# Half-array matmuls emitted in pairs on different halves: SSD heads alternate by chunk, attention heads go two at a time

## The chip, the cores and the metric

The kernel runs on one core of one Trainium2 chip. The metric is device microseconds from start to end. PE is TensorE, a 128 x 128 array; DVE is VectorE, ACT is ScalarE, POOL is GpSimd. Before the change three runs took 4758.9, 4764.99 and 4768.86 us, so the median is 4764.99.

## What is computed

Two blocks of a transformer-like model on 512 tokens of 1024 features, in float32. The first block has chunk attention (8 heads of 64), an S5 state-space mixer, memory attention and an expert layer (PEER). The second block has two layers; each mixes an SSD (2 groups of 8 heads of 64), latent attention (MLA, 8 heads), a gated delta rule (GDN) and a feed-forward layer. The three parts that the change touches, cut:

```python
# chunk attention: 64 features a head, a relative bias, a mask by chunks
s = jnp.einsum('bnqhd,bnkhd->bhnqk', qc, kb) * (ATT_HEAD_DIM ** -0.5)
p = jax.nn.softmax(where(..., s + bias, NEG_INF), axis=-1)
o = jnp.einsum('bhnqk,bnkhd->bnqhd', p, vb)
...
# SSD, chunks of 128: within a chunk, and from the states before it; p = 64 features a head
y_diag = jnp.einsum('bcgls,bgecls,bcsgep->bclgep', CB, L, X)
y_off = jnp.einsum('bclgn,bcgepn,bgecl->bclgep', Cc, h_prev, jnp.exp(A_cum))
...
# MLA: 128 features of a head's own keys, 64 rotary ones shared by the heads
sc = (jnp.einsum('bqhd,bkhd->bhqk', qn, k_nope) + jnp.einsum('bqhr,bkr->bhqk', qp, k_pe))
pr = jax.nn.softmax(jnp.where(kpos[None, :] <= qpos[:, None], sc * scale, -jnp.inf), axis=-1)
o = jnp.einsum('bhqk,bkhd->bqhd', pr, v)
```

## The kernel before

Activations lie with features on partitions, as tiles of 128 x 512 tokens. Most of PE's work is products with weights ("gemm"): weights and activations are split into two float32r parts, and each chunk of 128 features takes three matmuls of 512 columns (L162 to L164). A weight tile's parts are made by ACT (L140) and DVE (L141).

The order of each engine's instructions is set by a scheduler from the program's order, by its own model of the times. Parts that shall overlap are written as generators, which are run in turn (`interleave`, `lockstep`). Buffers are handed out in program order: PSUM has 5 banks called `s`, 2 called `g` and 1 called `o`; `w2` is a ring of 8 tiles of 128 x 512 for intermediate values.

Three places use half of the array.

**SSD** (`Layer.ssd`). For each group, 4 pairs `k` of heads. A head's running decays are put on all partitions (`rows`, L1419, four passes in the trace); ACT makes four Relu (L1488) and two exp (L1489, L1491), DVE multiplies (L1490, L1492) into `e1` and `e2`; then seven matmuls for the four chunks (L1496 within a chunk, L1498 from the state before it), whose stationary operand has 64 columns and whose output is half of the pair's bank `py`: partitions 0 to 63 for head 0, 64 to 127 for head 1.

**Chunk attention** (`attention_head`). Two heads of a pair are interleaved. Scores (L701) contract 64 features, which lie on partitions 0 to 63 or 64 to 127; values (L706) write half of the pair's bank.

**MLA** (`Layer.mla`). A loop over 8 heads. Scores of a block of queries are a full matmul (L1574, 128 features) and one over the 64 rotary features (L1575) that lie on one or the other half of the partitions. Values (L1581) use the whole array.

Both attentions call `causal_probs`. It works on four blocks of 128 queries in the order 3, 0, 2, 1, with 512, 128, 384 and 256 keys; blocks 0 and 2 share a bank. It computes all scores, then DVE's reductions for the maximum (L274, L276), then ACT's exp (L281) and DVE's reciprocal and product (L282, L283), then PE's transposes (L249) and ACT's copies to the tile `pT` (L289).

Of the kernel before, what the change touches and what calls it, by code (L numbers as in the profile page):

```python
# [11 lines left out]
F32 = mybir.dt.float32  # L12
# [3 lines left out]
AF = mybir.ActivationFunctionType  # L16
# [4 lines left out]
NEG = -1e30  # L21
# [28 lines left out]
class Builder:  # L50
    """Pools, constants and the operations that the stages share.

    Activations lie with features on partitions: a tensor of 1024 features is
    eight tiles of [128, 512 tokens]."""

    def __init__(self, tc, d, ctx):
# [3 lines left out]
        # whether the split of weights goes before all other work  # L60
# [31 lines left out]
    def psg(self):  # L92
        """In turn one of three banks; of two where attention takes the third."""
# [9 lines left out]
    def consts(self):  # L103
# [8 lines left out]
        # tri[s, l] = 1 where s <= l  # L112
# [6 lines left out]
    def rsqrt(self, out, x, scale, eps):  # L119
        """out = (scale * x + eps) ** -0.5 by Newton's steps, for small tiles."""  # L120
# [35 lines left out]
    def mm3(self, ps, wH, wL, xs, start=True, stop=True):  # L156
        """ps (+)= w.T @ x over the chunks, each operand in two parts."""
# [8 lines left out]
    def gemm(self, ap, xs, n=T, ps=None):  # L166
        """ap: weights, or their parts where they have been loaded already."""
# [6 lines left out]
    def colsum(self, ps, acc, n=T):  # L174
        """ps[:, tb] = the sum over partitions of acc, tokens on partitions."""
# [4 lines left out]
    def rowbc(self, ps, col, n=T):  # L180
        """ps[p, t] = col[t % 128, t // 128] on every partition."""
# [17 lines left out]
    def rstd_rows(self, srcs, width, eps=EPS, n=T, w2=None, pss=None):  # L199
        """A PSUM tile with the tokens' reciprocal root mean squares on every partition."""  # L200
# [10 lines left out]
    def rstd_tile(self, srcs, width, eps=EPS, out=None):  # L211
        """The same on chip, until the next norm or in out."""
# [33 lines left out]
    def transpose4(self, ps, src, n=T):  # L246
        """ps[:, tb*128:...] = the transposes of src's blocks of 128 columns."""
# [5 lines left out]
    def causal_probs(self, score, mask, scale, pT):  # L253
# [4 lines left out]
        n = [(i + 1) * P for i in range(4)]  # L258

        def blocks(tile):  # L260
            # a block's columns in three tiles: the last, the first and third, the second
            a, b, c = tile(), tile(), tile()
            return [b[:, :P], c[:, :2 * P], b[:, P:], a]

        order = (3, 0, 2, 1)
        ps = blocks(self.pss)
        for i in order:
            score(ps[i], i)
# [1702 lines left out]
```

## Time and profile before

| | |
|---|---|
| median of three runs | 4764.99 us (4758.9 to 4768.86) |
| span of the profiled execution | 4766.1 us |
| mean granted TensorE clock, core 0 | 0.987 of full |
| PE busy | 4705.0 us, 99% of the span |
| DVE busy | 2838.4 us, 60% |
| ACT busy | 1907.6 us, 40% |

The page gives no time of the profiled execution apart from its span, which lies 1.1 us above the median of the runs. A busy PE is one that has a matmul in flight; it doesn't say how much of the array works. An fp32 matmul stands in the trace as two passes, so a count there is twice the program's; a float32r matmul is one. The time of a row includes the way through the array, so what one pass costs is read from start to start.

### The profile page before, as it was taken

The page shows a single profiled execution, that of the slowest core. Times are in us where ns is not written, and L with a number is a line of the kernel's source. Part 1 is how long each engine was busy: PE and PEld are TensorE (multiplying, and loading weights), DVE is VectorE, ACT ScalarE, POOL GpSimd, SP SyncE. Part 2 cuts the span into 40 slices and gives each one's busy share as a digit, 9 for nine tenths or more (in the row PEclk, how much of TensorE's full clock was granted, in tenths as well). Part 3 has the DMA queues.
Part 4 walks back from the last instruction along what each step waited for, and adds up shares of the span by engine and source line. Part 5 has one row for each costly group of instructions (what it writes and reads, how often), then busy time and mean ns, then how long its engine had stood idle before and what let it go on. Part 6 is the DMA issues. An engine that isn't in the chain of part 4 may idle for free.

```text
span 4766.1 us, 59356 instructions
## 1 busy us (share of the span) xinstructions
PE 4705.0 (99%) x22296; PEld 3754.0 (79%) x22296; DVE 2838.4 (60%) x5744; ACT 1907.6 (40%) x3653; POOL 29.1 (1%) x59
## 2 busy tenths in 40 slices
PE   8999999999999999999999999999999999999998
PEld 6777788888888888887787678888877876888887
DVE  8655799665545555557776545544477764555434
ACT  3343348863222222323553433333345534333322
POOL 0000000000000000000000000000000000000000
PEclk9789999999999999999999999999999999999999
DMA  4222235564434443442254145423323531554332
GB/s 131 66 84 83 80 118 186 190 210 150 138 119 139 143 129 126 145 138 74 85 178 137 45 154 175 146 93 96 104 81 127 174 103 52 176 167 133 93 95 82
DMA packets 306048, 589.28 MB, mean 124 GB/s; under 512 B 60192, under 2 KB 147552, under 8 KB 303584
## 3 DMA queue, kind: packets, MB, share of 16 engines
q1 hardware_dynamic: 304480, 582.88, 37.7%
q0 software_dynamic: 1280, 2.59, 0.3%
q8 instruction: 176, 2.88, 0.2%
q14 instruction: 112, 0.92, 0.1%
HBM read 480.29 MB, written 105.09 MB: 123 GB/s over the span
## 4 chain that ended last, share of the span: by engine, by line
PE 91%; DVE 6%; DMA 1%; issue 1%; ACT 0%; SPq 0%; DVEq 0%; ACTq 0%
PE g L162 14%; PE g L163 14%; PE g L164 14%; PE o L163 6%; PE o L164 6%; PE o L162 6%; PE s L1170 5%; PE s L1171 5%; PE s L1169 5%; PE s L1116 3%; PE s L249 1%; DVE wL L141 1%; PE s L1575 1%; PE s L1574 1%; PE s L183 1%
## 5 line engine op out<-in xcount | busy, mean ns | idle before, releaser
L140 ACT ACTIVATE wH<-wr 128x1024 fp32r<-128x1024 f32 (+2 forms) x599 | 603.3, 1007 | 1305.3 <-PE g L163 794.9
L141 DVE TENSOR_TENSOR wL<-wr,wH 128x1024 fp32r<-128x1024 f32 (+2 forms) x599 | 692.2, 1156 | 444.4 <-ACT wH L140 428.6
L162 PE MATMUL g<-xH,wH 128*128 128x512 f32 (+1 forms) x2328 | 923.4, 397 | 16.7 <-ACT wH L140 13.7
L164 PE MATMUL g<-xH,wL 128*128 128x512 f32 (+1 forms) x2328 | 919.9, 395 | 6.6 <-DVE wL L141 6.5
L163 PE MATMUL g<-xL,wH 128*128 128x512 f32 (+1 forms) x2328 | 922.2, 396 | 0.0
L162 PEld LDWEIGHTS g<-xH,wH 128*128 128x128 f32 x2328 | 444.7, 191 | 118.9 <-ACT wH L140 14.0
L164 PEld LDWEIGHTS g<-xH,wL 128*128 128x128 f32 x2328 | 444.4, 191 | 106.8 <-DVE wL L141 10.9
L163 PEld LDWEIGHTS g<-xL,wH 128*128 128x128 f32 x2328 | 444.7, 191 | 95.3 <-issue 3.7
L164 PE MATMUL o<-xH,wL 128*128 128x512 f32 x1032 | 411.2, 398 | 1.5 <-DVE wL L141 1.5
L163 PE MATMUL o<-xL,wH 128*128 128x512 f32 x1032 | 412.4, 400 | 0.0
L162 PE MATMUL o<-xH,wH 128*128 128x512 f32 x1032 | 411.2, 398 | 0.0
L1170 PE MATMUL s<-WL,VH 128*128 128x512 f32 x1024 | 399.7, 391 | 1.3 <-DVE WL L141 1.3
L1169 PE MATMUL s<-WH,VH 128*128 128x512 f32 x1024 | 398.2, 391 | 0.0
L1171 PE MATMUL s<-WH,VL 128*128 128x512 f32 x1024 | 397.7, 390 | 0.0
L140 ACT ACTIVATE VH<-vr 128x1024 fp32r<-128x1024 f32 x128 | 132.3, 1056 | 542.9 <-PE s L1170 391.4
L1172 DVE TENSOR_TENSOR h<-h,s 128x512 f32<-128x512 f32 x256 | 174.1, 685 | 271.6 <-PE s L1171 271.5
L164 PE MATMUL g<-yH,wL 128*128 128x512 f32 x632 | 251.0, 397 | 2.3 <-DVE wL L141 2.3
L163 PE MATMUL g<-yL,wH 128*128 128x512 f32 x632 | 251.1, 397 | 0.7 <-DVE yL L230 0.7
L162 PE MATMUL g<-yH,wH 128*128 128x512 f32 x632 | 250.5, 397 | 0.0
L141 DVE TENSOR_TENSOR VL<-vr,VH 128x1024 fp32r<-128x1024 f32 x128 | 154.1, 1224 | 141.4 <-ACT VH L140 141.3
L164 PEld LDWEIGHTS o<-xH,wL 128*128 128x128 f32 x1032 | 194.6, 189 | 45.2 <-DVE wL L141 2.4
L162 PEld LDWEIGHTS o<-xH,wH 128*128 128x128 f32 x1032 | 194.5, 188 | 44.5 <-issue 2.2
(629 smaller groups left out, 7243.3 us busy)
## 6 DMA issues: line engine op xcount, KB each, us to landing
wr<-in_w_in SPq DMA_DIRECT2D x166, 512.0 KB, 3.6
wr<-in_pu SPq DMA_DIRECT2D x128, 512.0 KB, 4.2
vr<-in_pv SPq DMA_DIRECT2D x128, 512.0 KB, 3.7
gd<-G SPq DMA_DIRECT2D x16, 2048.0 KB, 6.5
gt<-gd SPq DMA_DIRECT2D x64, 512.0 KB, 5.3
wr<-in_w_o SPq DMA_DIRECT2D x64, 512.0 KB, 3.6
wr<-in_w_up SPq DMA_DIRECT2D x64, 512.0 KB, 3.5
wr<-in_w_dn SPq DMA_DIRECT2D x64, 512.0 KB, 3.5
```

Of the source, the lines that this page charges most:

```text
L140: nc.scalar.activation(H, src, AF.Copy)
L141: nc.vector.tensor_tensor(L, src, f32(H), op=OP.subtract)
L162: nc.tensor.matmul(ps, wH[:, k], xH, start=s, stop=False)
L163: nc.tensor.matmul(ps, wH[:, k], xL, start=False, stop=False)
L164: nc.tensor.matmul(ps, wL[:, k], xH, start=False, stop=e)
L183: self.nc.tensor.matmul(ps[:, tb * P:(tb + 1) * P], col[:, tb:tb + 1].to_broadcast([P, P]), self.ident, start=True, stop=True)
L249: self.nc.tensor.transpose(ps[:, tb * P:(tb + 1) * P], src[:, tb * P:(tb + 1) * P], self.ident)
L1116: nc.tensor.matmul(ps[:, j * P:(j + 1) * P], o2[:, k], og[:, j], start=True, stop=True)
L1169: nc.tensor.matmul(ps, VH[:, n], WH, start=k == 0, stop=False)
L1170: nc.tensor.matmul(ps, VH[:, n], WL, start=False, stop=False)
L1171: nc.tensor.matmul(ps, VL[:, n], WH, start=False, stop=k == 3)
L1172: nc.vector.tensor_tensor(h[n], h[n], ps, op=OP.add)
```

## The change

The SSD first prepares both heads of a pair, then goes through the chunks, and for each chunk and each of the two products issues head 0 and head 1 one after the other (L1523 for both). `causal_probs` takes two heads. For each block it issues the scores of both heads and right behind them, in the program, DVE's reductions of both; since blocks 0 and 2 share a bank, block 2's scores follow the reductions of block 0 there. The exp and the normalisation work in place, in the tiles that the reductions wrote. `attention_head` becomes `attention_pair`: scores on both row halves (L719), values on both column halves in turn (L727). The MLA takes its heads two at a time: full-array scores of both (L1604), then the rotary ones of both on the two row halves (L1608), values L1615. `qn`, `kn`, `vt` get 3 buffers in place of 2, the tiles `pT` 2 in place of 3. Comments are removed too, so line numbers shift; L274, L276, L281, L282, L283 and L289 become L282, L284, L292, L293, L294 and L300.

```diff
     def causal_probs(self, score, masks, scale, pTs):
-        ps = blocks(self.pss)
-        for i in order:
-            score(ps[i], i)
-        yield
...
-        s = blocks(self.w2)
+        ps, s, pt = blocks(self.pss), blocks(self.w2), blocks(self.pss)
+        mx, nmx, sm, ri = ([self.small([P, 4]) for _ in R2] for _ in range(4))
         for i in order:
             c = slice(i, i + 1)
-            nc.vector.tensor_tensor_reduce(out=s[i], in0=ps[i], in1=mask[:, T - n[i]:], scale=1.0,
...
+            score([ps(h, i) for h in R2], i)
+            for h in R2:
+                nc.vector.tensor_tensor_reduce(out=s(h, i), in0=ps(h, i), in1=masks[h][:, T - n[i]:], scale=1.0,
+                                               scalar=-3e38, op0=OP.add, op1=OP.max, accum_out=mx[h][:, c])
+                nc.vector.tensor_scalar(nmx[h][:, c], mx[h][:, c], -scale, None, op0=OP.mult)
+            if i == 0:
+                yield
+        yield
+        for h in R2:
+            for i in order:
+                c = slice(i, i + 1)
+                p = s(h, i)
+                nc.scalar.activation(p, p, AF.Exp, bias=nmx[h][:, c], scale=scale, accum_out=sm[h][:, c])
...
+            yield
+        for h in R2:
+            for i in order:
+                self.transpose4(pt(h, i), s(h, i), n[i])
...
 def attention_pair(B, qT, kT, vt, j, out, pool):
...
+    for k in range(4):
+        for h in R2:
+            lo = 64 * h
+            n = 64 * (2 * j + h)
+            nc.tensor.matmul(out[lo:lo + 64, k * P:], vt[:, k, n:n + 64], pTs[h][k], start=k == 0, stop=k == 3)
...
     def ssd(self, xs, xr, rs, decays, px, pool):
...
-                    for c in range(4):
-                        sl = slice(c * P, (c + 1) * P)
-                        o = py[64 * e:64 * e + 64, sl]
-                        nc.tensor.matmul(o, xd[:, c, 64 * hd:64 * hd + 64], e1[:, sl], start=True, stop=c == 0)
-                        if c:
-                            nc.tensor.matmul(o, st[c - 1][:, 64 * hd:64 * hd + 64], e2[:, sl],
-                                             start=False, stop=True)
+                    e1s.append(e1)
+                    e2s.append(e2)
+
+                for c in range(4):
+                    sl = slice(c * P, (c + 1) * P)
+                    for lhs, rhs, first in ((xd[:, c], e1s, True), (st[c - 1] if c else None, e2s, False)):
+                        for e in range(2):
+                            if lhs is not None:
+                                hd = 2 * k + e
+                                nc.tensor.matmul(py[64 * e:64 * e + 64, sl], lhs[:, 64 * hd:64 * hd + 64],
+                                                 rhs[e][:, sl], start=first, stop=c == 0 or not first)
...
     def mla(self, xs, gates, pool):
...
+            def score(pss, i):
+                sl, n = slice(i * P, (i + 1) * P), (i + 1) * P
+                for h in R2:
+                    nc.tensor.matmul(pss[h], qn[h][:, sl], kn[h][:, :n], start=True, stop=False)
+
+                for h in R2:
+                    lo = 64 * h
+                    nc.tensor.matmul(pss[h], qpe[lo:lo + 64, sl], kpe[lo:lo + 64, :n], start=False, stop=True)
```

How PE's order moves is shown at three places; a row gives line, operation, out<-in, and the shape of the output (partitions x columns), with what it waits for in brackets where it waits.

PE before, in the MLA's first layer: the scores of the first head (banks `s`; `kn` and `qn` are its keys and queries, `kpe` and `qpe` the rotary ones).

```order
L1574 MATMUL s_22120<-kn_22062,qn_22061 128x512 [waits PE_49]
L1575 MATMUL s_22120<-kpe_22013,qpe_22029 128x512
L1574 MATMUL s_22121<-kn_22062,qn_22061 128x128 [waits PE_49]
L1575 MATMUL s_22121<-kpe_22013,qpe_22029 128x128
L1574 MATMUL s_22121<-kn_22062,qn_22061 128x384
L1575 MATMUL s_22121<-kpe_22013,qpe_22029 128x384
L1574 MATMUL s_22122<-kn_22062,qn_22061 128x256
L1575 MATMUL s_22122<-kpe_22013,qpe_22029 128x256
```

PE after, at the same place: the first pair of heads, up to the third block of queries.

```order
L1604 MATMUL s_22164<-kn_22039,qn_22038 128x512 [waits PE_49]
L1604 MATMUL s_22165<-kn_22097,qn_22096 128x512
L1608 MATMUL s_22164<-kpe_21990,qpe_22006 128x512
L1608 MATMUL s_22165<-kpe_21990,qpe_22006 128x512
L1604 MATMUL s_22176<-kn_22039,qn_22038 128x128
L1604 MATMUL s_22177<-kn_22097,qn_22096 128x128 [waits PE_49]
L1608 MATMUL s_22176<-kpe_21990,qpe_22006 128x128
L1608 MATMUL s_22177<-kpe_21990,qpe_22006 128x128
L1604 MATMUL s_22196<-kn_22039,qn_22038 128x256 [waits DVE_49]
L1604 MATMUL s_22176<-kn_22039,qn_22038 128x384 [waits DVE_49]
L1604 MATMUL s_22177<-kn_22097,qn_22096 128x384 [waits DVE_49]
L1608 MATMUL s_22176<-kpe_21990,qpe_22006 128x384
```

Each block has its two full matmuls first and then its two rotary ones; the third block (384 columns) writes the banks of the second, `s_22176` and `s_22177`, and waits for DVE.

PE before, behind those scores: gemm rows for the next head's products (`g_22201`, `g_22221`) and the transposes (L249) of the normalised probabilities.

```order
L164 MATMUL g_22201<-cqH_21819,wL_22198 128x512
L162 MATMUL g_22201<-cqH_21825,wH_22197 128x512
L163 MATMUL g_22201<-cqL_21826,wH_22197 128x512
L249 MATMUL s_22161<-ident_65,w_4763_22146 128x128 [waits DVE_49]
L249 MATMUL s_22161<-ident_65,w_4763_22146 128x128 x3
L249 MATMUL s_22162<-ident_65,w_4764_22147 128x128 [waits DVE_49,PE_49]
L164 MATMUL g_22201<-cqH_21825,wL_22198 128x512
L162 MATMUL g_22221<-ckvH_21935,wH_22217 128x512
L163 MATMUL g_22221<-ckvL_21936,wH_22217 128x512
L164 MATMUL g_22221<-ckvH_21935,wL_22218 128x512
L249 MATMUL s_22163<-ident_65,w_4765_22148 128x128 [waits DVE_49]
L249 MATMUL s_22162<-ident_65,w_4764_22147 128x128 [waits Activation_49]
```

PE after, behind the last scores of the pair: the transposes of head 0's blocks 3 and 0 (`s_22232`, `s_22241`), gemm rows, and the transposes of its block 1 (`s_22250`) and of head 1 (`s_22255`).

```order
L249 MATMUL s_22232<-ident_65,w_4758_22170 128x128 [waits DVE_49]
L249 MATMUL s_22232<-ident_65,w_4758_22170 128x128 x3
L249 MATMUL s_22241<-ident_65,w_4762_22182 128x128 [waits DVE_49]
L164 MATMUL g_22303<-cqH_21789,wL_22300 128x512
L162 MATMUL g_22303<-cqH_21795,wH_22299 128x512
L163 MATMUL g_22303<-cqL_21796,wH_22299 128x512
L164 MATMUL g_22303<-cqH_21795,wL_22300 128x512
L162 MATMUL g_22303<-cqH_21801,wH_22299 128x512
L163 MATMUL g_22303<-cqL_21802,wH_22299 128x512
L164 MATMUL g_22303<-cqH_21801,wL_22300 128x512
L249 MATMUL s_22250<-ident_65,w_4766_22202 128x128 [waits DVE_49]
L249 MATMUL s_22250<-ident_65,w_4766_22202 128x128
```

Seven gemm rows stand ahead of the first transposes before, and none after; after, seven stand between the first head's block 0 and its block 1. Behind the pair's values come 48 gemm rows.

PE before, in the SSD: the end of one head and the gemm rows behind it.

```order
L1496 MATMUL s_18882<-w_4084_18906,xd_18697 64x128
L1498 MATMUL s_18882<-w_4085_18907,st_18746 64x128
L1496 MATMUL s_18882<-w_4084_18906,xd_18697 64x128
L1498 MATMUL s_18882<-w_4085_18907,st_18753 64x128
L164 MATMUL g_19402<-xH_18306,wL_19399 128x512
L162 MATMUL g_19402<-xH_18312,wH_19398 128x512
L163 MATMUL g_19402<-xL_18313,wH_19398 128x512
L164 MATMUL g_19402<-xH_18312,wL_19399 128x512
L162 MATMUL g_19402<-xH_18318,wH_19398 128x512
L163 MATMUL g_19402<-xL_18319,wH_19398 128x512
```

PE after: the third pair of a group. The first row of head 0 stands ahead of the `rows` (L1440) of the next pair, and the others alternate between head 0 (`w_4050`, `w_4051`) and head 1 (`w_4053`, `w_4054`).

```order
L1523 MATMUL s_18816<-w_4050_18820,xd_18673 64x128 [waits DVE_49]
L1440 MATMUL s_18859<-cumTH_18580,eye_14191 128x512 [waits PE_49]
L1440 MATMUL s_18859<-cumTL_18581,eye_14191 128x512
L1440 MATMUL s_18872<-cumTH_18580,eye_14191 128x512 [waits PE_49,Activation_49]
L1440 MATMUL s_18872<-cumTL_18581,eye_14191 128x512
L164 MATMUL g_19027<-xH_18294,wL_19024 128x512
L1523 MATMUL s_18816<-w_4053_18833,xd_18673 64x128 [waits DVE_49]
L1523 MATMUL s_18816<-w_4050_18820,xd_18673 64x128
L1523 MATMUL s_18816<-w_4053_18833,xd_18673 64x128 [waits Activation_49]
L1523 MATMUL s_18816<-w_4051_18821,st_18716 64x128
L1523 MATMUL s_18816<-w_4054_18834,st_18716 64x128
L1523 MATMUL s_18816<-w_4050_18820,xd_18673 64x128
```

The two heads' rows stand next to each other now, and few gemm rows are left between pairs. On PE as a whole the number of instructions of each line stays as it is.

## Rows read from the trace of the kernel before

**Rows 1.** The page, part 1: busy us, share of the span, instructions.

```profile
PE 4705.0 (99%) x22296; PEld 3754.0 (79%) x22296; DVE 2838.4 (60%) x5744; ACT 1907.6 (40%) x3653; POOL 29.1 (1%) x59
```

**Rows 2.** The page, part 4: the chain that ended last, by engine.

```profile
PE 91%; DVE 6%; DMA 1%; issue 1%; ACT 0%; SPq 0%; DVEq 0%; ACTq 0%
```

**Rows 3.** Windows: length, then PE, PEld, DVE, ACT, POOL busy, granted clock, DMA.

```profile
2270.00:2290.00 20.00, 20.00 (x109) 15.36 (x108) 13.38 (x21) 12.23 (x30) 0.00 (x0) 1.00 0.15 44
2660.00:2700.00 40.00, 40.00 (x166) 25.41 (x165) 20.44 (x72) 19.94 (x67) 0.00 (x0) 1.00 0.11 34
60.00:360.00 300.00, 289.74 (x1542) 218.01 (x1543) 190.40 (x654) 116.51 (x276) 21.50 (x40) 0.85 0.28 81
2240.00:2800.00 560.00, 555.89 (x2603) 419.84 (x2602) 375.17 (x759) 261.35 (x586) 1.26 (x1) 1.00 0.36 115
```

**Rows 4.** Timeline of PE, MLA values: start, us to the last end, line, shapes, count.

```profile
2651.96 2.32 PE L1581 MATMUL s<-pT,vt 128*128 128x512 f32 x8
2654.04 0.48 PE L164 MATMUL o<-ckvH,wL 128*128 128x512 f32 x1
```

**Rows 5.** Timeline of PE, one head of the SSD.

```profile
2267.97 0.65 PE L1496 MATMUL s<-w,xd 128*64 128x128 f32 x4
2268.46 0.38 PE L1498 MATMUL s<-w,st 128*64 128x128 f32 x2
2268.68 0.38 PE L1496 MATMUL s<-w,xd 128*64 128x128 f32 x2
...
2269.65 0.49 PE L1419 MATMUL s<-cumTH,eye 24*128 24x512 f32 x1
...
2270.76 0.50 PE L163 MATMUL g<-xL,wH 128*128 128x512 f32 x1
```

**Rows 6.** Timeline of PE, S5's alternating column halves and the matmul behind them.

```profile
106.92 1.15 PE L623 MATMUL s<-U,inj 128*64 128x64 f32 x32
108.00 0.50 PE L162 MATMUL g<-xH,wH 128*128 128x512 f32 x1
```

**Rows 7.** Timeline of PE, GDN's matmuls of 64 columns and the one behind.

```profile
2815.87 0.68 PE L1751 MATMUL s<-tt,a 64*64 64x64 f32 x8
2816.47 0.50 PE L164 MATMUL o<-xH,wL 128*128 128x512 f32 x1
```

**Rows 8.** Timeline of PE, S5's matmuls on the two row halves.

```profile
124.42 0.32 PE L651 MATMUL s<-x,car 64*128 64x64 f32 x1
124.44 0.32 PE L652 MATMUL s<-x,cai 64*128 64x64 f32 x1
```

**Rows 9.** Timeline of PE, one MLA head's scores, first rows, and the matmul behind.

```profile
2641.16 1.02 PE L1574 MATMUL s<-kn,qn 128*128 128x512 f32 x2
2642.11 1.12 PE L1575 MATMUL s<-kpe,qpe 64*128 64x512 f32 x2
...
2646.94 0.50 PE L163 MATMUL g<-cqL,wH 128*128 128x512 f32 x1
```

**Rows 10.** Timeline of DVE and ACT for the same head.

```profile
2643.28 0.69 DVE L274 CUSTOM_DVE_ANT_0 w<-s,cmask 128x512 f32<-128x512 f32 x1 [1.22 <-PE s L1575]
...
2644.01 0.15 DVE L276 TENSOR_SCALAR sm<-sm 128x1 f32<-128x1 f32 x1
2644.20 0.72 ACT L281 ACTIVATE w<-w,sm 128x512 f32<-128x512 f32 x1 [3.59 <-DVE sm L276]
...
2645.79 0.29 DVE L274 CUSTOM_DVE_ANT_0 w<-s,cmask 128x128 f32<-128x128 f32 x1 [1.62 <-PE s L1575]
...
2649.30 0.94 ACT L289 COPY pT<-s 128x128 f32<-128x128 f32 x5 [0.52 <-PE s L249]
```

**Rows 11.** Timeline of ACT in the SSD.

```profile
2270.41 1.14 ACT L1488 ACTIVATE w<-s,cum 128x128 f32<-128x128 f32 x4 [2.44 <-PE s L1419]
...
2272.31 1.17 ACT L1488 ACTIVATE w<-s,cum 128x128 f32<-128x128 f32 x4
2273.38 1.06 ACT L140 ACTIVATE wH<-wr 128x1024 fp32r<-128x1024 f32 x1
```

More of the change, by code (lines that the diff above doesn't have):

```diff
@@ L250, in transpose4, with causal_probs, at @@
                                      self.ident)
-    def causal_probs(self, score, mask, scale, pT):
+    def causal_probs(self, score, masks, scale, pTs):
         nc = self.nc
         n = [(i + 1) * P for i in range(4)]
+        order = (3, 0, 2, 1)
+        R2 = range(2)
         def blocks(tile):
-            a, b, c = tile(), tile(), tile()
-            return [b[:, :P], c[:, :2 * P], b[:, P:], a]
-        order = (3, 0, 2, 1)
-        ps = blocks(self.pss)
-        for i in order:
-            score(ps[i], i)
-        yield
-        mx, nmx, sm, ri = (self.small([P, 4]) for _ in range(4))
-        s = blocks(self.w2)
+            made = [{} for _ in R2]
+            def at(h, i):
+                t = {3: 0, 0: 1, 2: 1, 1: 2}[i]
+                if t not in made[h]:
+                    made[h][t] = tile()
+                x = made[h][t]
+                return {3: x, 0: x[:, :P], 2: x[:, P:], 1: x[:, :2 * P]}[i]
+            return at
+        ps, s, pt = blocks(self.pss), blocks(self.w2), blocks(self.pss)
+        mx, nmx, sm, ri = ([self.small([P, 4]) for _ in R2] for _ in range(4))
@@ L293, in prob_tiles @@
+    def prob_tiles(self, pool, bufs):
         t = self.t([P, 10 * P], F32, "pT", bufs, pool)
@@ L810, in heads @@
                 ps = B.t([P, T], F32, "o", 1, B.pp)
-                yield from interleave([attention_head(B, *pairs[j], vt, 2 * j + k, ps, pool) for k in range(2)], 2)
+                yield from attention_pair(B, *pairs[j], vt, j, ps, pool)
                 att.append(B.t([P, T], F32, "qk", 8, pool))
@@ new lines, in mla, with score @@
+        R2 = range(2)
+        for j in range(4):
+            qpe = t([P, T], "qpe", 2)
+            self.rope(qpe, B.gemm(B.d["w_uq2"][self.l, 8 + j], cq))
+            qn, kn, vt = [], [], []
+            for h in (2 * j, 2 * j + 1):
+                qn.append(t([P, T], "qn", 3))
+                kn.append(t([P, T], "kn", 3))
+                nc.scalar.copy(qn[-1], B.gemm(B.d["w_uq2"][self.l, h], cq))
+                nc.scalar.copy(kn[-1], B.gemm(B.d["w_ukv2"][self.l, h], ckv))
+                f = B.w2()
+                nc.scalar.copy(f, B.gemm(B.d["w_ukv2"][self.l, 8 + h], ckv))
+                ps = B.pss()
+                B.transpose4(ps, f)
+                vt.append(t([P, T], "vt", 3))
+                v.tensor_copy(vt[-1], ps)
+            pTs = [B.prob_tiles(pool, 2) for _ in R2]
+            def score(pss, i):
+                sl, n = slice(i * P, (i + 1) * P), (i + 1) * P
+                for h in R2:
+                    nc.tensor.matmul(pss[h], qn[h][:, sl], kn[h][:, :n], start=True, stop=False)
+                for h in R2:
+                    lo = 64 * h
+                    nc.tensor.matmul(pss[h], qpe[lo:lo + 64, sl], kpe[lo:lo + 64, :n], start=False, stop=True)
+            for _ in B.causal_probs(score, [S.cmask] * 2, scale, pTs):
+                pass
+            for h in R2:
+                ps = B.pss()
+                for k in range(4):
+                    nc.tensor.matmul(ps[:, k * P:], vt[h][:, k * P:(k + 1) * P], pTs[h][k],
+                                     start=k == 0, stop=k == 3)
+                H, L = B.hl("y")
+                B.split(ps, H, L)
+                out.append((H, L))
```

81 lines of the change are left out of this document (23 added, 58 removed).

## The prediction

> **What bounds the kernel now.** I read the page's busy shares first. TensorE (PE) is busy for 99% of the span, VectorE (DVE) 60%, ScalarE (ACT) 40% [rows 1], and the chain that ended last is 91% PE [rows 2]. So nearly everything PE gives up comes off the end, as long as it finds other work ready. Next I looked at the stages that are changed. In 20 us of the SSD, DVE works 13.4 and ACT 12.2; in 40 us of the latent attention (MLA), 20.4 and 19.9; PE is never idle there, and the clock is at its full level, 2.4 GHz, over the long stretches that hold both stages [rows 3]. DVE and ACT have room on average, but not much if their work is bunched. Only the stage of chunk attention and S5 (60 to 360 us) has a mean clock of 0.85.
>
> The span is 4766.1 us, the runs' median 4765.0; I subtract from 4765. Their spread is 10 us, about 0.2%: less than 9.5 us can't be told from no change.
>
> **What a half-array matmul costs now.** An fp32 matmul is two passes in the trace. In the MLA, four full-array `L1581` (512, 384, 256 and 128 columns, 8 passes) take 2651.96 to 2654.04: 2.08 us [rows 4]. One head's SSD matmuls step by 0.22 us for two passes of 128 columns on half the array [rows 5], which is also what two passes of 128 columns cost on the whole array by the first figure (2.08 x 2/20). Half an array is no faster; the other half idles.
>
> **Do two halves work at once?** The trace has a case: `L623` of S5 alternates the column halves, 32 passes of 64 columns. The next matmul starts 1.08 us after its start [rows 6], 34 ns for each pass, with the change of tile shape in it. Eight passes of 64 columns of `L1751` that don't alternate take 0.60 us, about 0.05 each after 0.2 for the change [rows 7]. So alternating passes go about two by two. For row halves: an `L651` and an `L652` on different halves and banks start 0.02 us apart [rows 8], though each runs for longer than that.
> The Trainium skill, "TensorE: Matmul & The Clock Gate", section "Part 3: Packing small matmuls", says that a weight load overlaps with running matmuls only where the row group differs; column halves share their rows. By that rule the SSD and `L706` would gain nothing, 26.6 us of the sum below. The 34 ns of `L623` speak against it, and the sum goes by the row. It remains a rival.
>
> **What a change of tile shape costs.** One MLA head's scores go from 2641.16 to 2646.94, 5.78 us, over eight instruction pairs that alternate whole array (`L1574`) and row half (`L1575`) [rows 9]. Their columns are those of two `L1581` groups, 4.16 us. The other 1.62 us are eight changes: 0.20 each.
>
> **The change, part by part.**
> SSD: 2 layers x 16 heads, 14 passes each [rows 5], 28 for a pair of heads; x 0.11 = 3.08 us. In the new order the first row of one head stands apart in 14 of 16 pairs; it costs its 0.22, and then the other half's seven rows bound the rest, 1.54: 1.76 in all, 1.32 less. 14 x 1.32 + 2 x 1.54 = **21.6 us**.
> MLA rope scores (`L1575`, now `L1608`): 16 heads x 2.08 = 33.3, all adjacent in pairs in the new order: half, **16.6**.
> Chunk attention scores (`L701`, now `L719`): 8 heads x 2.08 = 16.6 at full clock, adjacent too: **8.3**. Values (`L706`, now `L727`): the first row (512 columns, 0.83 us) of one head stands apart in every pair, so a pair of heads takes 0.83 + 2.08 in place of 4.16, 1.25 less, x 4 = **5.0**. Both run in the stretch with a clock of 0.85; their passes cost more there, up to 2 us together. I take the lower figure, since the clock may change as well.
> Changes of shape: counted down the two orders, 495 before and 415 after. 61 of the 80 are those between whole array and row halves (107 each way, now 76 and 77), nearly all in the MLA: 8 a pair of heads for 16. 61 x 0.20 = 12.2. The others lie at column halves: a head of the SSD leaves 0.14 us over its 14 passes when the rows of the next one start (2267.97 to 2269.65), so 19 x 0.15 = 2.9. Together **15.1**.
> Gross: 21.6 + 16.6 + 8.3 + 5.0 + 15.1 = 66.6 us.
>
> **New waits, MLA.** The third score (384 columns) now goes into the bank of the second, after DVE has reduced it. By the durations of before [rows 10]: the 512-column reduction and the small operation that ends at 2644.16 are 0.88 us together, the 128-column reduction 0.3. DVE does the 512 ones of both heads before the 128 ones, so the bank comes free some 2.1 us after the first scores end; PE has left by then the change, the 128-column scores (0.9 with their changes) and one 256-column `L1604` (0.42), 1.5 in all. Wait: 0.6.
> Then the transposes. Before, 7 gemm rows and more stand between scores and transposes and a single head's softmax follows. Now both heads' softmax must run at once, on ACT the exp of eight blocks (0.72 for 512 columns), on DVE eight reductions and eight normalisations behind one another. PE has two transposes' worth and 7 gemm rows (1.6 us) before it needs the last block of the first head. Following the queues of DVE and ACT with those durations, that block is ready 0.55 to 1.2 us after PE gets there; I take 0.9. The value products wait for ACT's copies out of PSUM (0.19 each), by up to 0.4; I take 0.3. Together 1.8 us for a pair of heads, x 8 = **14.4**. Behind PE's wait stand the next gemms, whose results are not needed for some 10 us (48 gemm rows follow a pair's values), so nothing else becomes late. Bounds: 0, if DVE and ACT run ahead, and double.
>
> **New waits, SSD.** A head costs ACT about 1.9 us (four Relu, two exp; from one `L1488` to the next, 2270.41 to 2272.31) [rows 11]. Before, 11 gemm rows stood between heads; now 0 to 5 stand between pairs, so the pairs of a group follow one another at ACT's pace. PE's own work for a pair is 2 x 1.11 (`L1419`, 2269.65 to 2270.76) + 1.76 + 0.3, and a gemm row or so, 4.5 to 5 us; ACT's 3.8, with a weight cast (1.06) up to 4.9. They are close, and what shows is the latency at the first and the last pair: about 1 us at each, 2 a group, 4 groups, **8 us**. Bounds: 0 and 16.
>
> **Sum:** 66.6 - 14.4 - 8 = 44 us; 4765 - 44 = **4721 us**.
>
> **Rivals.**
> A. The waits stay hidden: DVE and ACT run ahead of what I follow, and PE waits 0 to 8 us in all. For it: both work 50 to 70% of the time in these stages [rows 3]. Against it: the scores, the softmax that they need and the transposes stand next to each other in the new order, with 7 gemm rows to cover it. About 4699 us.
> B. Column halves run one after the other, for the rule above: 26.6 us are lost, and SSD's waits shrink by some 4: 4744.
> C. The softmax of two heads is a longer chain than I follow, for every hand-over between DVE and ACT adds to it, and a pair waits twice as long, 14 us more in all; so does the SSD, 8 more: 4743.
> D. Slower: in the MLA PE falls to the lower level of its clock, 1.2 GHz. Place: the stretch from 2639 to 2775 and its twin in the second layer, 136 us each, where PE would have new pauses and fewer rows busy. What speaks for it: between 60 and 360 us the clock is 0.85 in the mean, in a stage where gemms mix with short and half-array matmuls [rows 3]. Against it: both stretches ran at 1.00, with a pause at every change of shape. At half clock a stretch costs its own length more; from about 45 us of it in all the change loses. With half of both stretches, 136 us, 4857; with a quarter, 4789.
> E. The halves never run together, row halves neither: only the 15.1 us of changes against 22 of waits, 4772.
>
> **How the numbers follow.** Forecast (4709 to 4732) 0.50; A 0.20; B and C together 0.19; E 0.05; D 0.04; the last 0.02 is for a better clock in the first stage (by the mean of 0.85 some 90 of the 300 us ran at the lower level; a third of them at full clock would save 15). The range 4692 to 4750 reaches to A and past B and C, and leaves out D, E and the ends. Faster by over 0.2% in the forecast, A, nearly all of B and C: 0.88; within 0.2%: most of E and the tail of C, 0.07; slower: D and part of E, 0.05.
>
> **What would show it.** Right: the SSD rows now start two by two; `L1608` twins start within 0.05 us of one another; PE's busy time is lower by more than 40 us, with idle time before `L1604` (384 columns) named DVE and before `L249` named DVE of about 0.6 and 0.9 us a pair. Wrong: twins one after the other (B, E); PE's idle time above 40 us (C); a granted clock below 0.95 in 2639 to 2775 (D).

## The result, and the profile after

The changed kernel takes 4713.56 us (median; 4708.9 to 4717.0) against 4765.25 for the kernel before on the same chip: a ratio of 0.9887, with an interval of 0.9871 to 0.9903. That is 52 us less; 44 were forecast (4721), with a range of 4692 to 4750.

The page of the changed kernel, part 1 (busy us, share, instructions) and the line of part 4 (the chain that ended last, by engine); they answer to [rows 1, 2]:

```profile
PE 4638.6 (98%) x22296; PEld 3718.0 (79%) x22296; DVE 2838.5 (60%) x5744; ACT 1905.1 (40%) x3652; POOL 29.0 (1%) x59
...
PE 88%; DVE 8%; DMA 1%; ACT 1%; issue 1%; SPq 0%; DVEq 0%; ACTq 0%
```

PE's busy time falls by 66.4 us, the span by 54.8 (4766.1 to 4711.3), so some 12 us of what PE was freed from became idle time. Where the time went is read by following the same gemm matmul through both traces. It is the n-th in time of the gemm lines (L162 to L164, and the three lines of the expert layer's products, L1169 to L1171 before and L1190 to L1192 after), and it is taken at places where the difference stays flat for a while:

```
start of the n-th gemm matmul, us       before    after    difference
1150   behind chunk attention and S5      461.7    443.3   -18.4
7950   ahead of the first layer's SSD    2207.7   2189.9   -17.8
9100   behind it                         2571.1   2549.6   -21.6
9800   behind the first layer's MLA      2837.6   2805.7   -31.9
12450  ahead of the second layer's SSD   3521.6   3489.5   -32.1
13300  behind it                         3809.9   3765.3   -44.6
14000  behind the second layer's MLA     4062.5   4007.3   -55.2
```

So chunk attention and S5 gave 18 us, the MLA 10.3 and 10.6, the SSD 3.8 in the first layer and 12.5 in the second. The same code gave very unequal amounts in the two layers of the SSD; that is the first thing to explain. How far two executions of the same order can lie apart shows in `ssd_only` (experiment 1): its first stage is as before the change, and its 1150th gemm starts 3.7 us earlier all the same.

**The SSD.** The timeline of PE in the changed kernel, in the form of [rows 5] (L1523 are the matmuls of both heads, L1440 the `rows` of a head), at the first pair of the first layer:

```profile
2250.60 0.43 PE L1523 MATMUL s<-w,xd 128*64 128x128 f32 x2
2250.97 0.49 PE L1440 MATMUL s<-cumTH,eye 24*128 24x512 f32 x1
...
2252.51 0.54 PE L1523 MATMUL s<-w,xd 128*64 128x128 f32 x5
2252.78 0.27 PE L1523 MATMUL s<-w,st 128*64 128x128 f32 x1
2252.89 0.27 PE L1523 MATMUL s<-w,xd 128*64 128x128 f32 x1
2252.89 0.38 PE L1523 MATMUL s<-w,st 128*64 128x128 f32 x2
...
2253.77 0.48 PE L1523 MATMUL s<-w,st 128*64 128x128 f32 x3
2254.18 0.50 PE L164 MATMUL g<-xH,wL 128*128 128x512 f32 x1
```

Rows overlap now: an `xd` and an `st` row start at 2252.89 together. The 13 instructions (26 passes) from 2252.51 to 2254.18 take 1.67 us, where 26 passes one by one were 2.86. As forecast, one half's seven rows set that time, 1.54 and the change of shape.

A little later in the same group, PE between its other rows, with the wait ahead of a row in brackets:

```profile
2261.49 0.49 PE L164 MATMUL g<-xH,wL 128*128 128x512 f32 x1
2263.96 0.90 PE L1523 MATMUL s<-w,xd 128*64 128x128 f32 x5 [1.98 <-DVE w L1511]
2264.45 0.42 PE L1523 MATMUL s<-w,st 128*64 128x128 f32 x1
...
2264.66 0.63 PE L1523 MATMUL s<-w,st 128*64 128x128 f32 x2
...
2267.14 1.12 PE L249 MATMUL s<-ident,xs 128*128 128x128 f32 x4
2269.12 0.90 PE L1523 MATMUL s<-w,xd 128*64 128x128 f32 x5 [0.86 <-DVE w L1511]
...
2274.13 0.47 PE L162 MATMUL o<-xH,wH 128*128 128x512 f32 x1 [1.76 <-DVE wg L1318]
```

And windows of the changed kernel around it (length, then PE, PEld, DVE, ACT, POOL busy, granted clock, DMA):

```profile
2260.00:2262.00 2.00, 1.99 (x8) 1.03 (x7) 0.67 (x2) 1.88 (x4) 0.00 (x0) 1.00 0.00 0
2262.00:2264.00 2.00, 0.04 (x2) 0.04 (x2) 1.92 (x3) 2.00 (x8) 0.00 (x0) 0.70 0.00 0
2264.00:2268.00 4.00, 4.00 (x32) 3.53 (x32) 1.73 (x4) 2.23 (x6) 0.00 (x0) 0.50 0.44 131
2268.00:2272.00 4.00, 3.14 (x28) 2.85 (x26) 2.50 (x5) 0.00 (x0) 0.00 (x0) 0.50 0.00 0
2272.00:2274.00 2.00, 0.37 (x2) 0.00 (x0) 1.98 (x3) 0.00 (x0) 0.00 (x0) 0.74 0.00 0
2274.00:2280.00 6.00, 5.87 (x25) 4.82 (x26) 4.39 (x7) 2.85 (x5) 0.00 (x0) 1.00 0.00 0
```

PE waits 1.98 us at the third pair, 0.86 at the fourth and 1.76 behind the group, and within the first of these waits the clock goes to its lower level, 1.2 GHz, for some 10 us (a mean granted clock of 0.70 between 2262 and 2264, 0.74 between 2272 and 2274). In the row at 2264.45 a pass takes 0.42 us from end to end against 0.27 above. What PE waits for stands in the rows of DVE and ACT at that time:

```profile
2260.12 1.06 ACT L140 ACTIVATE wH<-wr 128x1024 fp32r<-128x1024 f32 x1 [0.23 <-PE g L163]
2261.08 0.61 ACT L1510 ACTIVATE w<-w 128x512 f32<-128x512 f32 x1
2261.60 1.12 ACT L1509 ACTIVATE w<-s,cum 128x128 f32<-128x128 f32 x4
```

```profile
2262.08 1.22 DVE L141 TENSOR_TENSOR wL<-wr,wH 128x1024 fp32r<-128x1024 f32 x1 [1.41 <-ACT w L1510]
2263.22 0.68 DVE L1511 TENSOR_TENSOR w<-w,cb 128x512 f32<-128x512 f32 x1
...
2267.24 0.75 DVE L1525 SCALAR_TENSOR_TENSOR xs<-xs,vec,s 128x512 f32<-128x512 f32 x1 [2.27 <-PE s L1523]
...
2268.38 0.69 DVE L1511 TENSOR_TENSOR w<-w,cb 128x512 f32<-128x512 f32 x1
```

ACT is at work nearly without a gap here, and has a weight cast (L140) between two of the SSD's operations. In DVE's order a weight split (L141) stands ahead of the product (L1511) for which PE waits. The trace names ACT's exp as what held the split up, but that exp ended at 2261.69, while PE's gemm of 2261.49 ended at 2261.98, just before the split starts; it may be the last reader of the weight tile that the split overwrites. At 2267.24 DVE's skip product (L1525) waits for PE in its turn, ahead of the fourth pair's products in DVE's queue.

This group also stands out in PE's order. From its first SSD row to its last, 11 gemm rows stand between the SSD's; in the other three groups there are 27, 32 and 31, and PE waits for nothing there. The prediction had 0 to 5 between pairs for every group. From the last row of one pair to the bulk of the next there are 7, 3 and 0 here, and 4 to 16 in the others.

**The MLA.** The timeline of PE in the changed kernel, first pair of the first layer (L1604 whole array, L1608 row halves); it answers to [rows 9]:

```profile
2626.02 1.88 PE L1604 MATMUL s<-kn,qn 128*128 128x512 f32 x4
2627.83 1.13 PE L1608 MATMUL s<-kpe,qpe 64*128 64x512 f32 x4
2628.89 0.71 PE L1604 MATMUL s<-kn,qn 128*128 128x128 f32 x4
2629.53 0.49 PE L1608 MATMUL s<-kpe,qpe 64*128 64x128 f32 x4
2629.95 2.36 PE L1604 MATMUL s<-kn,qn 128*128 128x256 f32 x6
2632.24 0.92 PE L1608 MATMUL s<-kpe,qpe 64*128 64x384 f32 x4
2633.09 0.70 PE L1604 MATMUL s<-kn,qn 128*128 128x256 f32 x2
2633.72 0.70 PE L1608 MATMUL s<-kpe,qpe 64*128 64x256 f32 x4
2634.35 0.77 PE L249 MATMUL s<-ident,w 128*128 128x128 f32 x5
...
2636.36 0.39 PE L164 MATMUL g<-cqH,wL 128*128 128x512 f32 x1
2636.93 1.71 PE L249 MATMUL s<-ident,w 128*128 128x128 f32 x12 [0.19 <-DVE w L294]
...
2643.57 0.71 PE L1546 MATMUL s<-w,rot 128*128 128x512 f32 x2
...
2674.85 0.71 PE L1546 MATMUL s<-w,rot 128*128 128x512 f32 x2
...
2706.00 0.71 PE L1546 MATMUL s<-w,rot 128*128 128x512 f32 x2
```

The scores of two heads take 8.33 us (2626.02 to 2634.35) in place of twice 5.78. Streaming explains 7.84: 4.16 for the whole-array ones, 2.08 for the rotary ones at half, eight changes at 0.20. The other 0.49 is the wait of the 384-column scores for DVE, hidden in the row at 2629.95, since earlier matmuls are still in flight. Another 0.34 lies ahead of the transposes at 2636.93 (the gemm at 2636.36 is through after 0.23), 0.16 ahead of the values. Together 1.0 us a pair. From the rotation (L1546) of one pair to that of the next, 2643.57 to 2674.85, it is 31.28 us here and 31.15 in the next pair; before the change it was 33.85:

```profile
2669.56 0.71 PE L1521 MATMUL s<-w,rot 128*128 128x512 f32 x2
```

```profile
2703.41 0.71 PE L1521 MATMUL s<-w,rot 128*128 128x512 f32 x2
```

### The profile page after: what moved, and what is told of

The parts are those of the page before. It is cut to its first block, busy times and chain, and to the rows that moved or that the text cites. A ratio compares the mean times of both kernels' runs of the same rounds, so it can differ in the third digit from the quotient of the medians.

```text
span 4711.3 us, 59345 instructions
## 1 busy us (share of the span) xinstructions
PE 4638.6 (98%) x22296; PEld 3718.0 (79%) x22296; DVE 2838.5 (60%) x5744; ACT 1905.1 (40%) x3652; POOL 29.0 (1%) x59
## 4 chain that ended last, share of the span: by engine, by line
PE 88%; DVE 8%; DMA 1%; ACT 1%; issue 1%; SPq 0%; DVEq 0%; ACTq 0%
PE g L162 13%; PE g L163 13%; PE g L164 13%; PE o L162 6%; PE o L163 6%; PE o L164 6%; PE s L1191 5%; PE s L1192 5%; PE s L1190 5%; PE s L1137 3%; DVE wL L141 1%; PE s L249 1%; PE s L183 1%; PE s L1615 1%; DMA vr<-in_pv 1%
## 5 line engine op out<-in xcount | busy, mean ns | idle before, releaser
L140 ACT ACTIVATE wH<-wr 128x1024 fp32r<-128x1024 f32 (+2 forms) x599 | 602.3, 1006 | 1328.8 <-PE g L163 810.9
L141 DVE TENSOR_TENSOR wL<-wr,wH 128x1024 fp32r<-128x1024 f32 (+2 forms) x599 | 692.6, 1157 | 444.0 <-ACT wH L140 425.8
L162 PE MATMUL g<-xH,wH 128*128 128x512 f32 (+1 forms) x2328 | 921.3, 396 | 16.1 <-ACT wH L140 12.4
L164 PE MATMUL g<-xH,wL 128*128 128x512 f32 (+1 forms) x2328 | 917.0, 394 | 3.0 <-DVE wL L141 3.0
L162 PEld LDWEIGHTS g<-xH,wH 128*128 128x128 f32 x2328 | 443.0, 190 | 117.7 <-ACT wH L140 13.3
L164 PEld LDWEIGHTS g<-xH,wL 128*128 128x128 f32 x2328 | 442.7, 190 | 101.5 <-DVE wL L141 6.4
L162 PE MATMUL o<-xH,wH 128*128 128x512 f32 x1032 | 411.9, 399 | 2.7 <-DVE wg L1318 1.8
L164 PE MATMUL o<-xH,wL 128*128 128x512 f32 x1032 | 411.2, 398 | 1.5 <-DVE wL L141 1.5
L1190 PE MATMUL s<-WH,VH 128*128 128x512 f32 x1024 | 398.2, 391 | 0.2 <-ACT WH L140 0.2
L1192 PE MATMUL s<-WH,VL 128*128 128x512 f32 x1024 | 397.6, 389 | 0.0
L140 ACT ACTIVATE VH<-vr 128x1024 fp32r<-128x1024 f32 x128 | 132.4, 1056 | 543.4 <-PE s L1191 385.1
L164 PE MATMUL g<-yH,wL 128*128 128x512 f32 x632 | 250.7, 397 | 3.0 <-DVE wL L141 3.0
L162 PE MATMUL g<-yH,wH 128*128 128x512 f32 x632 | 250.5, 397 | 0.0
L141 DVE TENSOR_TENSOR VL<-vr,VH 128x1024 fp32r<-128x1024 f32 x128 | 154.1, 1223 | 141.8 <-ACT VH L140 141.6
L162 PEld LDWEIGHTS o<-xH,wH 128*128 128x128 f32 x1032 | 194.4, 188 | 49.0 <-issue 5.2
L164 PEld LDWEIGHTS o<-xH,wL 128*128 128x128 f32 x1032 | 194.4, 188 | 45.9 <-DVE wL L141 2.4
```

The costliest lines, as they stand in the source:

```text
L140: nc.scalar.activation(H, src, AF.Copy)
L141: nc.vector.tensor_tensor(L, src, f32(H), op=OP.subtract)
L162: nc.tensor.matmul(ps, wH[:, k], xH, start=s, stop=False)
L164: nc.tensor.matmul(ps, wL[:, k], xH, start=False, stop=e)
L1190: nc.tensor.matmul(ps, VH[:, n], WH, start=k == 0, stop=False)
L1192: nc.tensor.matmul(ps, VL[:, n], WH, start=False, stop=k == 3)
```

## The experiments

The theory: halves that alternate run at once; what they save comes off the end, less PE's waits for DVE and ACT, which show at few places. The rivals: only the rearranged order and the fewer changes of tile shape count, or one stage's gain hangs on another's. Each kernel ran beside the kernel before on its own chip (4767.6, 4769.33 and 4769.51 us in the three groups), so times are compared by ratios, and within a group directly. The intervals of most ratios below overlap the changed kernel's (0.9871 to 0.9903), so what a part is worth is read from the traces, and the times only have to agree with it.

**1. The parts alone.** `ssd_only` is the kernel before with the new SSD; `att_only` has the new attentions and the old SSD.

```diff
# ssd_only: Layer.ssd as in the change; causal_probs, attention_head, mla as before
# att_only: the reverse
```

> The kernel before with the new SSD alone; both attentions are as before. If alternating column halves run at once, the SSD terms of the prediction hold: 21.6 + 2.9 us less and up to 8 us of waits, so 4741 to 4749 us; and if the loss that the changed kernel shows in the first group of the first layer (4.6 us of waits, and some 10 us at the lower clock) comes from the SSD's own order, it is here too, and the time is at the upper end, 4748. Rival: column halves run one after the other, and only the order of the work has changed: 4762 to 4770.

> The changed kernel with the SSD of before; both attentions in pairs. By the two traces, the stage of chunk attention and S5 gives 18 us and the MLA 25: 4722 us, and together with the SSD's part alone the two should add up to the whole change (52 us). Rival: the parts lean on one another (a shifted order in one stage makes the other's gain): the two alone add up to less than 45 us.

Measured: `ssd_only` 4753.93 us, ratio 0.9972 (0.9960 to 0.9983), 13.7 us less; `att_only` 4725.47, ratio 0.9911 (0.9894 to 0.9927), 42 us less. Together 56, the whole change 52: within these intervals (some 6 and 8 us either way) the parts add up. `ssd_only` lies a little above the upper end that I had named (4749). By its trace (the n-th gemm as above) its SSDs gave 3.6 and 12.5 us, as in the changed kernel: the loss in the first layer belongs to the SSD's own order.

**2. The same halves, in the MLA.**

```diff
                 for h in R2:
-                    lo = 64 * h
+                    lo = 0
                     nc.tensor.matmul(pss[h], qpe[lo:lo + 64, sl], kpe[lo:lo + 64, :n], start=False, stop=True)
```

> The changed kernel, but the rotary score matmuls of both heads of an MLA pair use the same row half (head 1 takes head 0's rotary queries, so its scores are not the reference's); order, number and shapes of the matmuls stay. If it is the different halves that let them run at once, 128 passes, half of 33.3 us, come back: 16.6 us, less up to 4 us of waits that they now cover, so 4726 to 4730 us. Rival: the MLA's gain is from fewer changes of tile shape alone: no difference, 4713.

Measured: 4722.54 us, ratio 0.9903 (0.9887 to 0.9920). Two rotations in its trace:

```profile
2645.45 0.71 PE L1546 MATMUL s<-w,rot 128*128 128x512 f32 x2
```

```profile
2677.80 0.71 PE L1546 MATMUL s<-w,rot 128*128 128x512 f32 x2
```

A pair takes 32.35 us against 31.15: 1.2 more, 9.5 over eight pairs. So different halves do run at once, and the rival falls. But only 1.2 of the 2.08 us a pair that the pairing takes off PE reach the end: with the scores longer, PE's waits in the pair are covered. And 33.85 to 32.35, 1.5 us a pair or 12 in all, is what is left for the fewer changes of shape: 8 changes at 0.19, close to the 0.20 of [rows 9].

**3. The SSD's heads one after the other.**

```diff
-                for c in range(4):
-                    sl = slice(c * P, (c + 1) * P)
-                    for lhs, rhs, first in (...):
-                        for e in range(2):
+                for e in range(2):
+                    for c in range(4):
+                        for lhs, rhs, first in (...):
```

> The changed kernel, both heads of an SSD pair prepared first, but the seven matmuls of head 0 emitted before the seven of head 1. If the alternation is what gains, the 21.6 us of the SSD come back, less what the first group lost to waits and the lower clock (up to 10 us): 4725 to 4735 us. Rival: the preparation of two heads together is what counts, or heads overlap without alternation: 4711 to 4716.

Measured: 4723.42 us, ratio 0.9903 (0.9887 to 0.9920). Against 0.9887 that is 7 to 8 us more. By the n-th gemm the SSDs of this kernel still give 3.6 and 4.6 us, where the changed kernel's gave 3.8 and 12.5, and in its trace there is no wait in the first group. So the alternation counts: some 8 us in the second layer, and in the first nothing of it is left. But this kernel does not take all of the overlap away. Where the two heads' rows stand next to each other, in 10 of the 16 pairs, they still overlap at the seam:

```profile
2252.81 0.65 PE L1523 MATMUL s<-w,xd 128*64 128x128 f32 x4
...
2253.95 0.44 PE L1523 MATMUL s<-w,xd 128*64 128x128 f32 x4
2254.17 0.27 PE L1523 MATMUL s<-w,st 128*64 128x128 f32 x1
...
2255.63 0.49 PE L1440 MATMUL s<-cumTH,eye 24*128 24x512 f32 x1
```

The four passes of the row at 2253.95 start within 0.22 us and not 0.44: two are head 0's, two are head 1's, which come later in the program. The 28 passes take 2.82 us, where 28 x 0.11 with one change of shape is 3.2. Some 0.4 us a pair, 4 in all, is overlap that is left; and around the SSD's rows and its `rows` there are 103 changes of shape for 126 before, 23 x 0.15 or 3.5 us. Together these are most of the 8 us that this kernel keeps.

**4. Chunk attention's scores on the same half.**

```diff
         for h in R2:
-            lo = 64 * h
+            lo = 0
             nc.tensor.matmul(pss[h], qT[lo:lo + 64, i * P:(i + 1) * P], kT[lo:lo + 64, :(i + 1) * P],
```

> The changed kernel, but the chunk attention's scores of both heads of a pair use the same row half (head 1 takes the queries and keys of head 0, so its scores are not the reference's); order, number and shapes of the matmuls stay. If the halves run at once there as in the MLA, half of 16.6 us at full clock comes back, 8 to 10 us with the clock of that stage, less what waits it covers: 3 to 10 us above the changed kernel. Rival: the stage's 18 us came from the order and the clock: within 2 us.

Measured: 4723.63 us, ratio 0.9905 (0.9886 to 0.9924). By the n-th gemm the stage gives 9.0 us in place of 18. A part of that is the clock: in the stage this execution spent 92.2 us at 1.2 GHz by the trace's record of the granted clock, the changed kernel's 88.7. `ssd_serial`, with the changed kernel's chunk attention and also 92.2 us, gives 15.9. So the scores' halves are worth some 7 us, of 8.3 forecast.

**5. ACT's pace in the SSD.** One Relu a head in place of four.

```diff
-                    for c in range(4):
-                        sl = slice(c * P, (c + 1) * P)
-                        nc.scalar.activation(e1[:, sl], R[:, sl], AF.Relu, scale=-1.0, bias=self.cum[:, c, j:j + 1])
+                    nc.scalar.activation(e1, R, AF.Relu, scale=-1.0, bias=self.cum[:, 0, j:j + 1])
```

> The changed kernel, but ACT makes one Relu of 512 columns with the first chunk's bias for each SSD head, in place of four of 128 with each chunk's (the SSD's result is not the reference's). ACT's time for a head falls from about 2.0 us to 1.6. If ACT's pace makes PE wait in the first group, those waits (4.7 us) shrink to half or less and the stretch at 1.2 GHz goes: 5 to 8 us below the changed kernel. Rival: it is the hand-over from engine to engine or DVE's order, not the pace: the waits stay above 3.5 us and the time within 2 us.

Measured: 4705.76 us, ratio 0.9859 (0.9840 to 0.9878). The window of the first group in the changed kernel, run once more beside other versions (`after_again`), and in this one:

```profile
2240.00:2280.00 40.00, 34.88 (x215) 25.42 (x214) 30.73 (x48) 22.95 (x60) 0.00 (x0) 0.92 0.12 39
```

```profile
2240.00:2280.00 40.00, 40.00 (x249) 29.16 (x248) 34.03 (x52) 22.14 (x38) 0.00 (x0) 1.00 0.15 45
```

With 0.4 us less of ACT's work a head, PE is never idle and the clock stays at 2.4 GHz. The first layer's SSD now gives 11.5 us, the second 12.7. So the first layer's missing 8 us are PE's waits in this group and the lower clock that goes with them. What removed them is not fully shown, for the scheduler also places things anew for this kernel: 16 gemm rows stand within the group in place of 11, and the weight split is no longer in its middle. ACT's own pace, the order's gemm rows and the split ahead of DVE's product are therefore not told apart here. A third buffer for weight tiles, which would free the split, wasn't tried.

**6. Two edits of the order.** `mla_defer` moves block 2's scores ahead of block 0's reductions; `ssd_ahead` prepares a pair before the matmuls of the pair ahead of it; `defer_ahead` has both. The changed kernel ran beside them.

```diff
# mla_defer
             score([ps(h, i) for h in R2], i)
-            for h in R2:
+            if i == 0:
+                yield
+                continue
+            for m in ((i,) if i != 2 else (0, 2)):
...
# ssd_ahead
+            ready = [prepare(0)]
             for k in range(4):
+                if k < 3:
+                    ready.append(prepare(k + 1))
```

> The changed kernel itself, beside the next three on the same chip: 0.987 to 0.990 of the kernel before. If the loss in the first SSD group of the first layer (waits of 2.0, 0.9 and 1.8 us before PE goes on, then about 10 us at 1.2 GHz) follows from the order, it is in this execution too; if it was chance, it is missing.

> The changed kernel, but the second block's reductions come behind the third block's scores in the program, as before the change, so that the 384-column scores don't wait for DVE. If half of the MLA's wait is that hand-over (0.5 of 1.0 us a pair in the trace of the changed kernel), 8 pairs give 4 us: 4 us below the changed kernel. Rival: the wait moves to the transposes, which now come 0.5 us earlier and need DVE's and ACT's chain all the same: within 1 us of the changed kernel.

> The changed kernel, with an SSD pair's rows, exp and products made one pair ahead of its matmuls in the program. If PE's waits in the first group come from DVE and ACT being asked late (the last pair's products stand behind the skip product, which waits for PE), they go, with the stretch at the lower clock: 5 to 10 us below the changed kernel. Rival: ACT's pace (about 2 us a head) is the limit, and too few gemm rows stand between pairs; then the waits stay somewhere in the group: within 2 us of the changed kernel.

> Both edits: if each does what its theory says, their gains add: 9 to 14 us below the changed kernel; by the rivals, within 3 us.

Measured: `after_again` 4716.28 us (4713.05 to 4717.66), ratio 0.9889 (0.9872 to 0.9905); `mla_defer` 4709.12 (4700.85 to 4712.22), 0.9870 (0.9854 to 0.9886); `ssd_ahead` 4716.08 (4711.13 to 4719.64), 0.9891 (0.9875 to 0.9908); `defer_ahead` 4706.17 (4704.12 to 4712.43), 0.9873 (0.9857 to 0.9890). Two rotations of `mla_defer`:

```profile
2645.55 0.71 PE L1548 MATMUL s<-w,rot 128*128 128x512 f32 x2
...
2676.25 0.70 PE L1548 MATMUL s<-w,rot 128*128 128x512 f32 x2
```

A pair takes 30.70 us in place of 31.15: the 0.45 of the hand-over is gone and doesn't come back at the transposes, 3.6 us in eight pairs. The medians differ by 7. By the n-th gemm the rest lies where the edit does not reach: in the first layer's SSD (5.2 us given, 3.5 in `after_again`) and ahead of the second layer's (where `after_again` loses 2.6), and in both places `after_again` spent 3.4 us more at 1.2 GHz. No execution of `mla_defer` is as slow as the fastest of `after_again`. `ssd_ahead` gains nothing that can be told: its window shows why.

```profile
2240.00:2280.00 40.00, 35.34 (x220) 24.82 (x219) 31.58 (x50) 22.80 (x59) 0.00 (x0) 0.96 0.12 38
```

PE is idle as long as in the changed kernel (4.7 us); only the time at the lower clock is shorter, and that differs without any edit of the SSD too (the last section). So asking one pair earlier does not help, though 22 gemm rows stand in the group now: more of these rows alone do not remove the waits, which speaks for the pace at which operands are made. The waits of the first group are in `after_again` too, so they belong to the order and not to chance.

**7. Relu on two engines.** `defer_ahead`, with every second head's Relu on DVE.

```diff
+                        if e == 0:
                             nc.scalar.activation(e1[:, sl], R[:, sl], AF.Relu, scale=-1.0, bias=...)
+                        else:
+                            v.tensor_scalar(e1[:, sl], R[:, sl], self.cum[:, c, j:j + 1], 0.0, op0=OP.subtract, op1=OP.min)
```

> The version with both edits (reductions of the second block deferred, SSD prepared one pair ahead), with the Relu of every second SSD head made by DVE instead (difference and minimum in one operation, from PSUM; the exp's sign follows). If ACT's pace is what is left in the first group, ACT has 1 us less a pair and the time is 3 to 6 us below that version, about 4700 us. Rival: DVE gets about 1.1 us more a pair and becomes what is waited for: no gain, or up to 4 us more.

Measured: 4720.77 us (4714.47 to 4727.09), ratio 0.9891 (0.9872 to 0.9909): slower than `defer_ahead` (0.9873) by some 8 us, where the rival had up to 4; the two intervals overlap, the executions' own ratios don't. Two windows of this kernel:

```profile
2280.00:2330.00 50.00, 50.00 (x244) 35.26 (x244) 36.80 (x63) 22.55 (x46) 0.00 (x0) 0.86 0.19 59
3480.00:3530.00 50.00, 47.46 (x230) 34.92 (x232) 41.61 (x82) 23.81 (x48) 0.00 (x0) 0.93 0.17 53
```

In the first the clock falls behind the group. PE's 2.5 us of idle time in the second are a wait of 2.9 us that the kernel before has at the same gemm; DVE is as busy in the changed kernel's window. New in the second layer are waits of 1.2 us for DVE's product and of 1.9 us behind the second group, also named DVE, and 14 us at 1.2 GHz. So the waits there are DVE's, as the rival had it; but the order changed too (62 gemm rows in one group), and how much of the loss each made is not shown. `defer_ahead` lies 10 us below the changed kernel on the same chip, 4706.17 against 4716.28, and the two sets of executions don't touch; from `mla_defer` alone (4709.12) it can't be told.

## Why the prediction was right, step by step

- **Halves run at once.** Right, for row halves (experiments 2 and 4; in the trace the two heads' passes of L1608 start 0.01 us apart) and column halves (experiment 3 and the rows at 2252.51). The Trainium skill's rule on weight loads ("TensorE: Matmul & The Clock Gate", "Part 3: Packing small matmuls"), read so that column halves gain nothing, differs from the measurement, and the measurement decides: 26 passes on alternating column halves took 1.67 us, change of shape included. That reading went further than the section of the Trainium skill, whose table gives 2.38 times for three column tiles; two halves come to 1.7 times here (2.86 to 1.67 us).
- **MLA.** Forecast 12.2 + 16.6 - 14.4 = 14.4 us; measured 10.3 + 10.6 = 21. The changes of shape are as forecast (12). The term that was mis-sized is the wait: 1.0 us a pair and not 1.8. The hand-over at the 384-column scores was 0.49 (forecast 0.6), the transposes 0.34 (0.9), the values 0.16 (0.3). The chain of the two softmaxes was reckoned too slow.
- **Chunk attention.** Forecast 8.3 + 5.0 = 13.3; measured 18, but the change itself is worth less than forecast, and the clock made up for it. By the trace's record of the granted clock, the time at 1.2 GHz ahead of the 1150th gemm differs from execution to execution. A pass steps by 0.21 us there (2264.45, 2264.66) and by 0.11 at 2.4 GHz (2252.78, 2252.89), so half of that time is taken off here, as an estimate of what the lower level cost:

```
                                1150th gemm   at 1.2 GHz   less half of it
before                                461.7        102.4             410.5
ssd_only (chunk attention old)        457.9         95.6             410.1
after                                 443.3         88.7             398.9
after_again                           443.5         88.7             399.2
att_only                              441.1         81.9             400.1
mla_same_half                         447.6         95.6             399.8
ssd_serial                            445.8         92.2             399.7
att_same_half (scores on one half)    452.7         92.2             406.6
```

So the change is worth some 11 us: 7 from the scores' halves (8.3 forecast) and 4 for the values and the rest (5.0). The other 7 of the 18 are 13.7 us less at 1.2 GHz, which the sum had put at nothing and the prediction's last line of chances, at 0.02, had named. The old order has only two executions here, so it is not shown that the new one shortens that time.

- **SSD.** Forecast 21.6 + 2.9 - 8 = 16.5; measured 3.8 + 12.5 = 16.3. The gross terms hold: the second layer, where PE does not wait, gave 12.5 of 12.25 forecast for one layer. The loss of 8 us has the forecast size by luck. It doesn't lie at two waits in each of four groups: it is all in one group, and by the profile (PE waits of 4.6 us, then 10 us at half clock) about half is waits and half the clock, which the sum did not have there. In four other executions with this order (`after_again`, `ssd_only`, `mla_same_half`, `att_same_half`) the waits are 5.1 to 5.3 us and the time at 1.2 GHz 3.4 to 6.8. With the waits and half of the busy time at 1.2 GHz added back, the first layer's SSD gives 12 us in all five, as the second does.
- **Rivals.** A (waits hidden) is half right in the MLA. B, C and E are out. D named the clock in the MLA, where it stayed at 1.00; the same mechanism struck in the SSD, on a small scale.
- **The total.** 44 forecast, 52 measured. The path is as forecast: halves overlap, fewer changes of shape, less the waits for DVE and ACT. That the sum came so close is in part luck, for the MLA's wait was sized too large, chunk attention's gain too large, and the clock of its stage gave some 7 us that the sum did not have.

## What to carry to other kernels

Half-array matmuls are worth pairing on different halves where they stand next to each other: their time halves. But count the changes of tile shape too (0.2 us each here); grouping like shapes gave 12 us in the MLA, the overlap 9.5. Then ask, stage by stage, whether the engines that feed the matmuls keep up at the new pace: where they don't, the saved time turns into a wait, and the clock can cost almost as much again, here 1.7 to 3.8 us on top of 5 us of waits.

## What was not expected of the hardware

In the first SSD group, one wait of 2 us in an otherwise busy stretch (PE 0.04 us of 2 busy between 2262 and 2264) went with a fall to 1.2 GHz that lasted 10 us, in which PE ran paired half-array rows and waited again; the clock was back at 2.4 GHz about 2273, within another pause. The wait does not set how long the lower level lasts. `mla_defer` has the same SSD order and waits of 2.0, 1.1 and 2.0 us in that group, and spent 3.4 us there:

```profile
2240.00:2280.00 40.00, 34.99 (x226) 25.58 (x226) 31.62 (x52) 23.25 (x63) 0.00 (x0) 0.96 0.13 40
```

The mean clock of this window was 0.92 in `after_again`, and 0.96 in `ssd_ahead` with waits of 1.1, 1.3 and 2.3 us. Nor does a fall need a pause just ahead of it: in `split_relu` PE had worked without one since 2267, was busy for all of 2280 to 2330, and the mean clock of that window was 0.86.
